# A two-layer decoder trunk in fp32 on one core: other addresses for activation halves and weight halves in SBUF

## The chip, the core and the metric

The program runs on one core of one Trainium2 chip. Its time is the device time of one execution in microseconds (us), as the median of 3 runs; the kernel before takes 2720.65 us (2719.96 to 2721.87).

## What is computed

Two decoder layers on 256 tokens of width 2048, everything in fp32. Each layer is a token mixer, a SwiGLU block and a per-layer input, with RMS norms ahead of and behind them:

```
for i in range(2):
    mix = ssd_mixer(rmsnorm(h), ...) if i == 0 else fox_mixer(rmsnorm(h), ...)
    h = h + rmsnorm(mix)
    ff = (silu(hn @ w_gate) * (hn @ w_up)) @ w_down        # hn = rmsnorm(h), hidden 5632
    h = h + rmsnorm(ff)
    h = h + sigmoid(h @ w_pgate) * rmsnorm(p[i] @ w_proj)  # p[i]: 256 tokens x 256
```

Layer 0's mixer is a state-space one (input projection 2048 x 10304, a convolution, a chunked scan, output projection 4096 x 2048); layer 1's is attention with 16 heads of 128 (input projection 2048 x 6160, output projection 2048 x 2048). There are 125 million weights, used once each.

## The kernel before

**Layout.** Activations lie transposed: 128 channels on the partitions, 256 tokens along the free axis, so 16 tiles hold one activation of width 2048. An fp32 product is made of three products of rounded halves: an activation is split into `x` hi and `x` lo, a weight into `wh` and `wl` (type fp32r), and hi·wh + lo·wh + hi·wl is summed in PSUM.

**Weight stages.** `emit_stage` (from L167) loads one stage of weights, up to 128 x 1024 words, into `raw` (L177, SyncE's DMA queue), casts it to `wh` on ScalarE (L189) and subtracts on VectorE to get `wl` (L194). There are 6 buffers of `raw` and 4 each of `wh` and `wl`.

**Products.** `unit` (from L209) walks through the stages of up to 6 output tiles. The common form is a pair: a *wide* product (L256) that loads 128 columns of `wh` as the stationary operand and streams 512 columns of one activation tile, hi and lo one behind the other, and a *narrow* one (L258) that loads `wl` and streams the 256 columns of hi. While a product streams, the weights of the following one are loaded into TensorE (PEld in the profile). Two other forms exist. In *separate* units (`sep`, L251 to L253; the last unit of every output projection) each pair is three products of 256 columns. In *token* units (`tok`, L245 to L247; the values of the attention layer) the activation is the stationary operand and 412 or 416 columns of weights stream.

**Small products.** L444 to L448 (`filler`) project the per-layer input, in the gaps that the norms leave. Plain fp32 products of the scan, the attention scores and the transposes stand between the units.

**What sets the order.** Python code emits the work unit by unit; lists of small steps (`bg`) are popped between stages; a scheduler then orders the instructions of each engine. Pools decide the addresses: they lie one behind the other in SBUF in the order in which they are opened (L68 to L79). Three pools, `gap_l`, `gap_x` and `gap`, hold nothing but 16, 24 and 56 words of padding (L43 to L45).

**Addresses before.** Counted in fp32 words and modulo 64, and adding up the pools in their order: every tile of `wh` starts at word 8 and every tile of `wl` at 24 (4 x 1024 words and 16 of padding later). The 16 tiles of `h` hold 40 words beside their 16 x 256, so with 24 words of padding every tile of `x` starts at 24 too, and so do the tiles `a` (SwiGLU), `xq` (second half of the scan's output) and `xb` (input of layer 1). The lo half follows the hi half directly, at 24 again, since a half has 4 x 64 words.

**Tiles that the change moves.** `praw` holds `p[i]` (L422) until it is split into `psp` (`part`, L426). `pp` (16 tiles for the projected per-layer input), `gz` (10 buffers, L766) and `pn` (4 buffers, L784) are the per-layer input's and update's own. `dtT`, `adT`, `dtk`, `acT`, `nega` are the scan's step sizes (L820 to L825). `q` and `k` of four heads at a time lie in 12 buffers `qk` (L1340, L1347); the attention outputs `ots` are 16 tiles `x` (L1264), written in `values` (L1319).

Of the kernel before, what the change touches and what calls it, by code (L numbers as in the profile page):

```python
# [41 lines left out]
TAIL_WIDE = 2  # L42
GAP_L = 16  # L43
GAP_X = 24
GAP_A = 56  # L45

_VEC = {}
# [12 lines left out]
def tile_trunk(ctx, tc, a, out):  # L60
# [13 lines left out]
    gap_x = pool(ctx, "gap_x")  # L74
    xp = pool(ctx, "xp", bufs=16)
    ev = pool(ctx, "ev", bufs=2)
# [14 lines left out]
    ones = cp.tile([P, P], F32, name="ones")  # L91
    mhalf = cp.tile([P, 2], F32, name="mhalf")

    def col(name, c=0, n=P):
# [72 lines left out]
    def emit_stage(a_ins=None, v_ins=None):  # L167
        i = len(emitted)
        cols, r, kc, n = stages[i]

        def view(t):
            return t[:, :kc * n].rearrange("p (c n) -> p c n", n=n)

        raw = wp.tile([P, SW], F32, tag="raw", name=f"raw{i}", bufs=RAWB)
        o = 0
        for W, c0, w in cols:
            nc.sync.dma_start(  # L177
                out=view(raw)[:, :, o:o + w],
                in_=W[r:r + kc * P, c0:c0 + w].rearrange("(c p) n -> p c n", p=P))
            o += w  # L180
        wh = whp.tile([P, SW], F32R, tag="wh", name=f"wh{i}", bufs=WB)
        wl = wlp.tile([P, SW], F32R, tag="wl", name=f"wl{i}", bufs=WB)
        if a_ins is None:
            a_ins, turn_a[0] = turn_a[0], None
        with ExitStack() as order:
            for ins in [a_ins] + lag[0]:
                order.enter_context(after(ins))
            lag[:] = [lag[1], []]
            low_a[0] = A.copy(out=wh[:, :kc * n], in_=raw[:, :kc * n])  # L189
        with ExitStack() as order:  # L190
            for ins in [v_ins] + turn:
                order.enter_context(after(ins))
            turn.clear()
            low[0] = V.tensor_tensor(out=wl[:, :kc * n], in0=raw[:, :kc * n],  # L194
                                     in1=wh.bitcast(F32)[:, :kc * n], op=sub)
        emitted.append((view(wh), view(wl), kc))
# [12 lines left out]
    def unit(rhs, evac, tok=False, pre=None, pops=1, late=(), merge=1, look=LOOK, sep=False):  # L209
# [10 lines left out]
        while k0 < K:  # L220
# [12 lines left out]
            with after(p0):  # L233
                p = None
                for t in range(nt):
                    with after(p if ordered else None):
                        for wh, wl, kc, kb in held:
                            for c in range(kc):
# [16 lines left out]
                                else:  # L255
                                    PE.matmul(accs[t], lhsT=wh[:, c, t * P:(t + 1) * P],  # L256
                                              rhs=x.rearrange("p a n -> p (a n)"), start=st, stop=False)
                                    last = PE.matmul(accs[t][:, :T], lhsT=wl[:, c, t * P:(t + 1) * P],  # L258
# [135 lines left out]
    A.dma_start(out=hx[0][:, :T + NCH], in_=a["x0"])  # L394
    x00 = xp.tile([P, 2, T], F32R, tag="x", name=nm("x"))
    V.tensor_scalar(out=x00[:, 0, :], in0=h[0], scalar1=hx[0][:, T:T + 1], scalar2=None, op0=mult)
# [7 lines left out]
    for _ in range(WARM):  # L404
        PE.matmul(wps[:, :P], lhsT=ones, rhs=ones, start=True, stop=True)

    def newx():
        return xp.tile([P, 2, T], F32R, tag="x", name=nm("x"))

# [10 lines left out]

    def load_p(i, mp):
        pr = mp.tile([P, 2, T], F32, tag="praw", name=f"praw{i}")  # L422
        G.dma_start(out=pr, in_=a[f"pT{i}"].rearrange("(c p) n -> p c n", p=P))
        pts.clear()

        def part(c):  # L426
            t = mp.tile([P, 2, T], F32R, tag=f"psp{c}", name=f"psp{i}_{c}")
            placed(pr[:, c, :], t)
            pts.append(t)
        bg.extend((noop, noop, noop, lambda: part(0), lambda: part(1)))  # L430
# [157 lines left out]
    def tail(i, mpx, m, pp, mk_next):  # L588
# [3 lines left out]
        with ExitStack() as st:  # L592
# [38 lines left out]
            for half in range(2):  # L631
                acts = [ap_.tile([P, 2, T], F32R, tag="a", name=nm("a")) for _ in range(HALF)]
                c0 = 0
# [38 lines left out]
        xs2 = [newx() for _ in range(NCH)]  # L672
        next_xs = mk_next() if mk_next is not None else None
        r0 = post_norm(filler(pp, (2, 3)))

# [88 lines left out]
        def e3(t, acc, c0):  # L764
            c = c0 + t
            gz[c] = pn.tile([P, T], F32, tag="gz", name=nm("gz"), bufs=10)  # L766
            gather(acc, gz[c])
# [12 lines left out]
        for u, (n, todo) in enumerate(zip(OUT0, (pops0, pops1, pops2, pops3))):  # L780
            last = u == len(OUT0) - 1
            up = None
            if u == 0:
                up = mk_update(lambda: pn.tile([P, T], F32, tag="pn", name=nm("pn"), bufs=4), m,  # L784
                               f"ffn_post{i}", None, xs2, r0)
# [27 lines left out]
    with ExitStack() as ys:  # L813
        yp = pool(ys, "yp", side="right")
        y = [yp.tile([P, T], F32, name=f"y{c}") for c in range(32)]
        with ExitStack() as st:
            sp = pool(st, "sp")
            dp = pool(st, "dp", space=bass.MemoryType.DRAM)
            acd = dp.tile([NH, T], F32, name="acd")
            dtT = sp.tile([NH, T], F32, name="dtT")  # L820
            adT = sp.tile([NH, T], F32, name="adT")
            dtk = sp.tile([P, 4, NH], F32, name="dtk")
            acT = sp.tile([NH, T], F32, name="acT")
            bias3 = sp.tile([P, 3, NH], F32, name="bias3")
            nega = sp.tile([NH, 1], F32, name="nega")  # L825
            cbm = [sp.tile([P, 384], F32, name=f"cbm{g}") for g in range(NG)]
            s2s = ExitStack()
            s2 = pool(s2s, "s2")
            bT = [s2.tile([P, T], F32, name=f"bT{g}") for g in range(NG)]
            wdt.append(s2.tile([P, NCH * NH], F32, name="wdt"))  # L830
# [272 lines left out]
            def z_unit(g, pops):  # L1103
                S = {}

                def ev_z(t, acc):
# [3 lines left out]
                    if t == 0:  # L1110
                        S["ss"] = yp.tile([P, T], F32, tag="gss", name=nm("gss"), bufs=1)
                        if g == 0:
# [32 lines left out]
            def ysplit(c):  # L1145
                if c not in yts:
                    yts[c] = newx() if c < 16 else xq.tile([P, 2, T], F32R, tag="xq",
                                                           name=nm("xq"))
                    placed(y[c], yts[c])
# [18 lines left out]
        def m0():  # L1168
            if not st0:
# [6 lines left out]
                st0["m"] = [st0["mp"].tile([P, T], F32, name=f"m0_{c}") for c in range(NCH)]  # L1176
                st0["pp"] = [st0["mp"].tile([P, T], F32, name=f"pp0_{c}") for c in range(NCH)]
                load_p(0, st0["mp"])
            return st0["m"]
# [4 lines left out]
    def mk_next():  # L1184
        p_ = pool(xr_s, "xb")
        return [p_.tile([P, 2, T], F32R, tag=f"xb{c}", name=nm("xb")) for c in range(NCH)]
    nxt = tail(0, st0["s"], st0["m"], st0["pp"], mk_next)
# [75 lines left out]
    bg.extend((f1, noop, f2, noop, f3))  # L1263
    ots = [newx() for _ in range(FH)]  # L1264

    RNG = ((0, P), (P, 384))

    def quad_tasks(hds, q, k):
# [50 lines left out]
        def values():  # L1319
            pss = [misc(), misc()]  # L1320

            def mm(i, b):
# [6 lines left out]
                   hds[-1] == FH - 1)  # L1329
            for i in range(4):  # L1330
                split(pss[i // 2][:, (i % 2) * T:(i % 2 + 1) * T], ots[hds[i]])

# [6 lines left out]
    for u in range(4):  # L1339
        q = [fp.tile([P, T], F32, tag="qk", name=nm("q"), bufs=12) for _ in range(4)]  # L1340

# [4 lines left out]
        unit(lambda k: nxt[k], ev_q)  # L1346
        kk = [fp.tile([P, T], F32, tag="qk", name=nm("k"), bufs=12) for _ in range(4)]  # L1347

# [13 lines left out]
    def m1():  # L1362
        if not st1:
# [5 lines left out]
            st1["m"] = [st1["mp"].tile([P, T], F32, name=f"m1_{c}") for c in range(NCH)]  # L1369
            st1["pp"] = [st1["mp"].tile([P, T], F32, name=f"pp1_{c}") for c in range(NCH)]  # L1370
            load_p(1, st1["mp"])
        return st1["m"]
# [72 lines left out]
```

## Time and profile before

| | |
|---|---|
| median of 3 runs | 2720.65 us |
| time of the profiled execution | 2720.78 us |
| its span | 2719.0 us |
| PE (matmul) busy | 2711.1 us, 100% of the span |
| PEld (weight load) busy | 2410.5 us, 89% |
| DVE (VectorE) busy | 1905.3 us, 70% |
| ACT (ScalarE) busy | 1480.7 us, 54% |
| DMA | 519.59 MB, 191 GB/s |

A matmul's end is modelled in the profile and its pipeline overlaps the next one, so a "busy" TensorE says little. What counts is the distance from the start of one product to the start of the next. It is read from the timeline (columns: start in us, length in us, engine, line, operation, output and inputs, how many were merged) or from a table of stretches: a stretch, its length, then the busy time of an engine and in brackets how many of its instructions ran in it, one or two of which reach in over the edge.

### The profile page before, as it was taken

The page shows a single profiled execution, that of the slowest core. Times are in us where ns is not written, and L with a number is a line of the kernel's source. Part 1 is how long each engine was busy: PE and PEld are TensorE (multiplying, and loading weights), DVE is VectorE, ACT ScalarE, POOL GpSimd, SP SyncE. Part 2 cuts the span into 40 slices and gives each one's busy share as a digit, 9 for nine tenths or more (in the row PEclk, how much of TensorE's full clock was granted, in tenths as well). Part 3 has the DMA queues.
Part 4 walks back from the last instruction along what each step waited for, and adds up shares of the span by engine and source line. Part 5 has one row for each costly group of instructions (what it writes and reads, how often), then busy time and mean ns, then how long its engine had stood idle before and what let it go on. Part 6 is the DMA issues. An engine that isn't in the chain of part 4 may idle for free.

```text
span 2719.0 us, 43137 instructions
## 1 busy us (share of the span) xinstructions
PE 2711.1 (100%) x16342; PEld 2410.5 (89%) x16342; DVE 1905.3 (70%) x3147; ACT 1480.7 (54%) x2455; POOL 48.8 (2%) x106
## 2 busy tenths in 40 slices
PE   9999999999999999999999999999999999999999
PEld 8888888889888888888898998889888888888898
DVE  8888888755976645666668656766976646666577
ACT  6577677554655444545456544555654444445454
POOL 0000000000000000000000000000000000000000
PEclk9999999999999999999999999999999999999999
DMA  7666666565666656666556676655666566656655
GB/s 265 186 203 189 191 202 188 159 215 168 188 206 193 193 194 192 193 179 202 199 161 198 184 215 188 185 156 168 203 199 196 189 199 190 198 176 201 202 162 167
DMA packets 262657, 519.59 MB, mean 191 GB/s; under 512 B 17408, under 2 KB 44192, under 8 KB 262448
## 3 DMA queue, kind: packets, MB, share of 16 engines
q1 hardware_dynamic: 258784, 504.54, 60.2%
q0 software_dynamic: 3520, 12.15, 1.5%
q8 instruction: 128, 2.10, 0.3%
q14 instruction: 81, 0.66, 0.1%
q10 hardware_dynamic: 144, 0.14, 0.0%
HBM read 514.58 MB, written 2.18 MB: 190 GB/s over the span
## 4 chain that ended last, share of the span: by engine, by line
PE 97%; DVE 1%; ACT 1%; issue 1%; DMA 0%; DVEq 0%; ACTq 0%
PE acc L256 56%; PE acc L258 29%; PE acc L253 1%; PE acc L252 1%; PE acc L251 1%; PE acc L247 1%; PE acc L246 1%; PE acc L245 1%; PE mi L1012 1%; DVE wl L194 1%; ACT E L992 1%; PE mi L1277 0%; PE mi L1325 0%; ACT wh L189 0%; PE acc L444 0%
## 5 line engine op out<-in xcount | busy, mean ns | idle before, releaser
L256 PE MATMUL acc<-x,wh 128*128 128x512 f32 x4992 | 1673.4, 391 | 0.9 <-DVE gz L285 0.8
L194 DVE TENSOR_TENSOR wl<-raw,wh 128x1024 fp32r<-128x1024 f32 (+4 forms) x1020 | 1169.4, 1152 | 694.0 <-ACT wh L189 688.9
L189 ACT CAST wh<-raw 128x1024 fp32r<-128x1024 f32 (+4 forms) x1020 | 1006.4, 993 | 934.0 <-PE acc L256 800.0
L258 PE MATMUL acc<-x,wl 128*128 128x256 f32 x4992 | 1305.2, 278 | 0.9 <-DVE wl L194 0.7
L256 PEld LDWEIGHTS acc<-x,wh 128*128 128x128 f32 x4992 | 921.8, 188 | 181.8 <-issue 1.3
L258 PEld LDWEIGHTS acc<-x,wl 128*128 128x128 f32 x4992 | 923.0, 188 | 26.4 <-DVE wl L194 3.4
L256 PE MATMUL acc<-a,wh 128*128 128x512 f32 x1232 | 417.5, 389 | 0.0
L258 PE MATMUL acc<-a,wl 128*128 128x256 f32 x1232 | 335.2, 276 | 0.0
L256 PEld LDWEIGHTS acc<-a,wh 128*128 128x128 f32 x1232 | 229.8, 188 | 46.2
L258 PEld LDWEIGHTS acc<-a,wl 128*128 128x128 f32 x1232 | 231.3, 188 | 2.1
L256 PE MATMUL acc<-xb,wh 128*128 128x512 f32 x512 | 176.6, 392 | 0.0
L284 ACT COPY tb<-acc 128x256 f32<-128x256 f32 x400 | 140.5, 370 | 48.6 <-PE acc L258 20.9
L258 PE MATMUL acc<-xb,wl 128*128 128x256 f32 x512 | 142.4, 279 | 0.0
L256 PEld LDWEIGHTS acc<-xb,wh 128*128 128x128 f32 x512 | 95.6, 188 | 19.2
L258 PEld LDWEIGHTS acc<-xb,wl 128*128 128x128 f32 x512 | 96.2, 188 | 0.8 <-issue 0.2
L256 PE MATMUL acc<-xq,wh 128*128 128x512 f32 x224 | 76.3, 389 | 0.0
L908 DVE SCALAR_TENSOR_TENSOR g<-xr,vec,g 128x256 f32<-128x256 f32 x144 | 63.5, 478 | 11.6 <-ACT g L905 11.4
L285 DVE TENSOR_TENSOR g<-acc,tb 128x256 f32<-128x256 f32 x171 | 65.1, 416 | 0.4
L258 PE MATMUL acc<-xq,wl 128*128 128x256 f32 x224 | 61.7, 276 | 0.0
L992 ACT ACTIVATE E<-ab,bias 128x128 f32<-128x128 f32 x192 | 59.9, 393 | 2.5 <-DMA ab<-acd 2.5
L308 DVE TENSOR_TENSOR ssb<-ssb,sq 128x256 f32<-128x256 f32 x120 | 50.6, 422 | 12.4 <-ACT sq L307 8.7
L344 POOL TENSOR_TENSOR rs<-ms,mhalf 128x2 f32<-128x2 f32 x18 | 22.6, 1255 | 1965.7 <-DVE ms L341 1965.7
(228 smaller groups left out, 2160.1 us busy)
## 6 DMA issues: line engine op xcount, KB each, us to landing
raw<-down SPq DMA_DIRECT2D x176, 512.0 KB, 4.2
raw<-ssd_in SPq DMA_DIRECT2D x144, 512.0 KB, 4.5
raw<-gate SPq DMA_DIRECT2D x128, 512.0 KB, 4.2
raw<-up SPq DMA_DIRECT2D x128, 512.0 KB, 4.4
raw<-fox_in SPq DMA_DIRECT2D x64, 512.0 KB, 4.2
raw<-gate SPq DMA_DIRECT2D x64, 384.0 KB, 3.3
raw<-up SPq DMA_DIRECT2D x64, 384.0 KB, 3.5
raw<-ssd_out SPq DMA_DIRECT2D x40, 512.0 KB, 4.1
```

The source lines that it names most:

```text
L189: low_a[0] = A.copy(out=wh[:, :kc * n], in_=raw[:, :kc * n])
L194: low[0] = V.tensor_tensor(out=wl[:, :kc * n], in0=raw[:, :kc * n], in1=wh.bitcast(F32)[:, :kc * n], op=sub)
L245: PE.matmul(o, lhsT=xh, rhs=wh[:, c, :], start=st, stop=False)
L246: PE.matmul(o, lhsT=xh, rhs=wl[:, c, :], start=False, stop=False)
L247: last = PE.matmul(o, lhsT=x[:, 1, t * P:(t + 1) * P], rhs=wh[:, c, :], start=False, stop=sp)
L256: PE.matmul(accs[t], lhsT=wh[:, c, t * P:(t + 1) * P], rhs=x.rearrange("p a n -> p (a n)"), start=st, stop=False)
L258: last = PE.matmul(accs[t][:, :T], lhsT=wl[:, c, t * P:(t + 1) * P], rhs=x[:, 0, :], start=False, stop=sp)
L284: i = A.copy(out=tb[:np_], in_=acc[:np_, T:2 * T])
L285: took[0] = (i, V.tensor_tensor(out=o, in0=acc[:np_, :T], in1=tb[:np_], op=add))
L308: last_v[0] = V.tensor_tensor(out=acc, in0=acc, in1=sq, op=add)
L908: V.scalar_tensor_tensor(out=c, in0=xr[:, k:k + T], scalar=col(f"conv_w{k}", cc), in1=c, op0=mult, op1=add)
L992: A.activation(E[:, i, b * P:(b + 1) * P], ab[:, i, lo:lo + P], AF.Relu, scale=-1.0, bias=bias3[:, b, h0 + i:h0 + i + 1])
```

## The change

All addresses below are in fp32 words modulo 64.

- `xp`, `act`, `xq`, `xb` and `psp` tiles grow from 512 to 576 words (`ROOM_X`), and the lo half starts 308 words behind the hi half (`LOW_X`; 308 = 256 + 52). The wide product's moving operand becomes two runs of 256 words (`[[308, 2], [1, 256]]`) where it was one run of 512.
- `gap_l` grows from 16 to 48 words, and `wl` tiles from 1024 to 1088 words, used from the 4th. So `wl` now starts at 60 (8 + 48 + 4), the hi halves at 56, the lo halves at 44, and `wh` stays at 8: `wh` lies 16 and `wl` 4 words past hi.
- To make room: `p[i]` is loaded by two DMAs into `m[14]` and `m[15]`, which are written only later; `pp[8:16]` is allocated when the SwiGLU tiles are gone; `pn` and `gz` share 11 buffers in place of 4 and 10; `dtk` lives in `rpe`, the sums of squares of the scan's norm in `ssp`; `dtT`, `adT`, `acT`, `nega` live in a pool that closes earlier; `q` and `k` lie in the room of the `x` tiles, four heads a slot group, and the attention outputs come into the same slots after them (`newx` takes a slot number).

```
-GAP_L = 16
+GAP_L = 48
 GAP_X = 24
 GAP_A = 56
+LOW_X = 308
+ROOM_X = 576
+SHIFT_L = 4
+ROOM_L = 64
...
-    xp = pool(ctx, "xp", bufs=16)
+    xp = pool(ctx, "xp")
...
+    def halves(pool_, **kw):
+        t = pool_.tile([P, ROOM_X], F32R, **kw)
+        return bass.AP(t.tensor, t.offset, [list(t.ap[0]), [LOW_X, 2], [1, T]])
+
+    slot = iter(range(1 << 20))
+
+    def newx(c=None):
+        c = next(slot) % NCH if c is None else c
+        return halves(xp, tag=f"x{c}", name=nm("x"))
...
-        wl = wlp.tile([P, SW], F32R, tag="wl", name=f"wl{i}", bufs=WB)
+        wl = wlp.tile([P, SW + ROOM_L], F32R, tag="wl", name=f"wl{i}", bufs=WB)
+        wl = wl[:, SHIFT_L:SHIFT_L + SW]
...
-                                    PE.matmul(accs[t], lhsT=wh[:, c, t * P:(t + 1) * P],
-                                              rhs=x.rearrange("p a n -> p (a n)"), start=st, stop=False)
+                                    PE.matmul(accs[t].rearrange("p (a n) -> p a n", a=2),
+                                              lhsT=wh[:, c, t * P:(t + 1) * P], rhs=x,
+                                              start=st, stop=False)
...
-    def load_p(i, mp):
-        pr = mp.tile([P, 2, T], F32, tag="praw", name=f"praw{i}")
-        G.dma_start(out=pr, in_=a[f"pT{i}"].rearrange("(c p) n -> p c n", p=P))
+    def load_p(i, mp, pr):
+        for c in range(2):
+            G.dma_start(out=pr[c], in_=a[f"pT{i}"][c * P:(c + 1) * P, :])
...
-                acts = [ap_.tile([P, 2, T], F32R, tag="a", name=nm("a")) for _ in range(HALF)]
+                acts = [halves(ap_, tag="a", name=nm("a")) for _ in range(HALF)]
...
+        pp_ = pool(mpx, f"ppb{i}", side="right")
+        pp.extend(pp_.tile([P, T], F32, name=f"ppb{i}_{c}") for c in range(8, NCH))
...
-            gz[c] = pn.tile([P, T], F32, tag="gz", name=nm("gz"), bufs=10)
+            gz[c] = pn.tile([P, T], F32, tag="gz", name=nm("gz"), bufs=11)
...
-                up = mk_update(lambda: pn.tile([P, T], F32, tag="pn", name=nm("pn"), bufs=4), m,
+                up = mk_update(lambda: pn.tile([P, T], F32, tag="gz", name=nm("pn"), bufs=11), m,
...
-            dtk = sp.tile([P, 4, NH], F32, name="dtk")
+            dtk = rpe.rearrange("p (a n) -> p a n", n=NH)
...
-                        S["ss"] = yp.tile([P, T], F32, tag="gss", name=nm("gss"), bufs=1)
+                        S["ss"] = ssp
...
-    ots = [newx() for _ in range(FH)]
+    ots = {}
...
+                ots[hds[i]] = newx(hds[i])
                 split(pss[i // 2][:, (i % 2) * T:(i % 2 + 1) * T], ots[hds[i]])
...
-        q = [fp.tile([P, T], F32, tag="qk", name=nm("q"), bufs=12) for _ in range(4)]
+        qk = [xp.tile([P, ROOM_X], F32, tag=f"x{4 * u + j}", name=nm("qk")) for j in range(4)]
+        q = [o[:, :T] for o in qk]
...
-        kk = [fp.tile([P, T], F32, tag="qk", name=nm("k"), bufs=12) for _ in range(4)]
+        kk = [o[:, T:2 * T] for o in qk]
```

**What it does to the order.** TensorE's and SyncE's lists hold the same instructions in the same order before and after, and VectorE's and ScalarE's differ at one place. That place is the last attention quad (`values` of heads 12 to 15), where ScalarE casts the hi halves of four head outputs (L289, L305 after) and the weight stages that follow (L189, L204 after). ScalarE's list before (`x` is a head's output tile, `mi` the PSUM tile it comes from, `wh` and `raw` a weight stage):

```order
1555 L189 CAST wh_19318<-raw_19316 128x768
1556 L289 CAST x_16998<-mi_19280 128x256
1557 L289 CAST x_16999<-mi_19280 128x256
1558 L289 CAST x_17000<-mi_19281 128x256
1559 L189 CAST wh_19336<-raw_19334 128x768
1560 L289 CAST x_17001<-mi_19281 128x256
1561 L189 CAST wh_19354<-raw_19352 128x768
```

And ScalarE's list after, at the same rows:

```order
1555 L204 CAST wh_19297<-raw_19295 128x768
1556 L305 CAST x_19271<-mi_19256 128x256
1557 L305 CAST x_19274<-mi_19256 128x256
1558 L305 CAST x_19265<-mi_19255 128x256
1559 L305 CAST x_19268<-mi_19255 128x256
1560 L204 CAST wh_19315<-raw_19313 128x768
1561 L204 CAST wh_19333<-raw_19331 128x768
```

The fourth cast of a head has moved ahead of one weight cast; VectorE's subtractions move in the same way.

GpSimd's list, where the per-layer input of layer 0 is loaded (`pT` in memory; `rs` are the small powers of the norms), before:

```order
82 L344 TENSOR_TENSOR rs_5669<-ms_5667,mhalf 128x2
83 L344 TENSOR_TENSOR rs_6081<-ms_6079,mhalf 128x2
84 L423 DMA praw_6632<-pT 128x2x256
85 L344 TENSOR_TENSOR rs_7723<-ms_7721,mhalf 128x2
86 L344 TENSOR_TENSOR rs_8365<-ms_8363,mhalf 128x2
```

And after:

```order
82 L360 TENSOR_TENSOR rs_5661<-ms_5659,mhalf 128x2
83 L360 TENSOR_TENSOR rs_6072<-ms_6070,mhalf 128x2
84 L436 DMA m_14_6605<-pT 128x256
85 L436 DMA m_15_6606<-pT 128x256
86 L360 TENSOR_TENSOR rs_7706<-ms_7704,mhalf 128x2
87 L360 TENSOR_TENSOR rs_8348<-ms_8346,mhalf 128x2
```

One DMA has become two, at the same place between the same powers; the same happens in layer 1.

More of the change, by code (lines that the diff above doesn't have):

```diff
@@ L394, in tile_trunk @@
     A.dma_start(out=hx[0][:, :T + NCH], in_=a["x0"])
-    x00 = xp.tile([P, 2, T], F32R, tag="x", name=nm("x"))
+    x00 = newx()
     V.tensor_scalar(out=x00[:, 0, :], in0=h[0], scalar1=hx[0][:, T:T + 1], scalar2=None, op0=mult)
@@ L405, in tile_trunk @@
         PE.matmul(wps[:, :P], lhsT=ones, rhs=ones, start=True, stop=True)
-    def newx():
-        return xp.tile([P, 2, T], F32R, tag="x", name=nm("x"))
     rwide = cp.tile([P, T], F32, name="rwide")
@@ L419, in tile_trunk @@
     pts, lo_done, held_pp = [], set(), []
-    def load_p(i, mp):
-        pr = mp.tile([P, 2, T], F32, tag="praw", name=f"praw{i}")
-        G.dma_start(out=pr, in_=a[f"pT{i}"].rearrange("(c p) n -> p c n", p=P))
+    def load_p(i, mp, pr):
+        for c in range(2):
+            G.dma_start(out=pr[c], in_=a[f"pT{i}"][c * P:(c + 1) * P, :])
         pts.clear()
         def part(c):
-            t = mp.tile([P, 2, T], F32R, tag=f"psp{c}", name=f"psp{i}_{c}")
-            placed(pr[:, c, :], t)
+            t = halves(mp, tag=f"psp{c}", name=f"psp{i}_{c}")
+            placed(pr[c], t)
             pts.append(t)
@@ L819, in tile_trunk @@
             acd = dp.tile([NH, T], F32, name="acd")
-            dtT = sp.tile([NH, T], F32, name="dtT")
-            adT = sp.tile([NH, T], F32, name="adT")
-            dtk = sp.tile([P, 4, NH], F32, name="dtk")
-            acT = sp.tile([NH, T], F32, name="acT")
+            dtk = rpe.rearrange("p (a n) -> p a n", n=NH)
             bias3 = sp.tile([P, 3, NH], F32, name="bias3")
-            nega = sp.tile([NH, 1], F32, name="nega")
             cbm = [sp.tile([P, 384], F32, name=f"cbm{g}") for g in range(NG)]
@@ L828, in tile_trunk @@
             s2 = pool(s2s, "s2")
+            dtT, adT, acT = (s2.tile([NH, T], F32, name=n) for n in ("dtT", "adT", "acT"))
+            nega = s2.tile([NH, 1], F32, name="nega")
             bT = [s2.tile([P, T], F32, name=f"bT{g}") for g in range(NG)]
@@ L1146, in ysplit @@
                 if c not in yts:
-                    yts[c] = newx() if c < 16 else xq.tile([P, 2, T], F32R, tag="xq",
-                                                           name=nm("xq"))
+                    yts[c] = newx() if c < 16 else halves(xq, tag="xq", name=nm("xq"))
                     placed(y[c], yts[c])
@@ L1176, in m0 @@
                 st0["m"] = [st0["mp"].tile([P, T], F32, name=f"m0_{c}") for c in range(NCH)]
-                st0["pp"] = [st0["mp"].tile([P, T], F32, name=f"pp0_{c}") for c in range(NCH)]
-                load_p(0, st0["mp"])
+                st0["pp"] = [st0["mp"].tile([P, T], F32, name=f"pp0_{c}") for c in range(8)]
+                load_p(0, st0["mp"], st0["m"][14:])
             return st0["m"]
@@ L1185, in mk_next @@
         p_ = pool(xr_s, "xb")
-        return [p_.tile([P, 2, T], F32R, tag=f"xb{c}", name=nm("xb")) for c in range(NCH)]
+        return [halves(p_, tag=f"xb{c}", name=nm("xb")) for c in range(NCH)]
     nxt = tail(0, st0["s"], st0["m"], st0["pp"], mk_next)
@@ L1369, in m1 @@
             st1["m"] = [st1["mp"].tile([P, T], F32, name=f"m1_{c}") for c in range(NCH)]
-            st1["pp"] = [st1["mp"].tile([P, T], F32, name=f"pp1_{c}") for c in range(NCH)]
-            load_p(1, st1["mp"])
+            st1["pp"] = [st1["mp"].tile([P, T], F32, name=f"pp1_{c}") for c in range(8)]
+            load_p(1, st1["mp"], st1["m"][14:])
         return st1["m"]
```

## Prediction

> **What bounds the kernel now.** I read the page first: whose work the span consists of.
>
> ```profile
> span 2719.0 us, 43137 instructions
> ...
> PEclk9999999999999999999999999999999999999999
> ...
> PE 97%; DVE 1%; ACT 1%; issue 1%; DMA 0%; DVEq 0%; ACTq 0%
> ...
> L256 PE MATMUL acc<-x,wh 128*128 128x512 f32 x4992 | 1673.4, 391 | 0.9 <-DVE gz L285 0.8
> L258 PE MATMUL acc<-x,wl 128*128 128x256 f32 x4992 | 1305.2, 278 | 0.9 <-DVE wl L194 0.7
> L256 PE MATMUL acc<-a,wh 128*128 128x512 f32 x1232 | 417.5, 389 | 0.0
> L256 PE MATMUL acc<-xb,wh 128*128 128x512 f32 x512 | 176.6, 392 | 0.0
> L256 PE MATMUL acc<-xq,wh 128*128 128x512 f32 x224 | 76.3, 389 | 0.0
> ```
>
> The chain that ended last is TensorE's for 97% of the span, at a full granted clock, with almost no idle time ahead of its products. There are 4992 + 1232 + 512 + 224 = 6960 pairs of a wide and a narrow product. So the time is the number of products times the distance from one start to the next. I looked for that distance in stretches in which only pairs run, by counting the narrow product L258 (PE and PEld: busy us and count).
>
> ```profile
> 540.00:640.00 100.00, 80.65 (x295) 55.16 (x294) 1.00 0.63 207
> 760.00:1222.00 462.00, 369.68 (x1358) 254.73 (x1357) 1.00 0.63 193
> 1968.00:2420.00 452.00, 361.72 (x1328) 249.13 (x1328) 1.00 0.63 193
> ```
>
> 462 us / 1357 and 452 / 1328 are 0.340 us a pair, over 2600 pairs with hardly an exception. A pair streams 768 columns, so this *clean beat* is 0.4427 ns a column: 226.7 ns for a wide product, 113.3 ns for a narrow one. At it the 6960 pairs need 2366 us. It isn't kept everywhere. The same two lines, in the scan's input projection:
>
> ```profile
> 299.77 0.40 PE L256 MATMUL acc<-x,wh 128*128 128x512 f32 x1
> 300.01 0.28 PE L258 MATMUL acc<-x,wl 128*128 128x256 f32 x1
> 300.12 0.40 PE L256 MATMUL acc<-x,wh 128*128 128x512 f32 x1
> ...
> 300.47 0.40 PE L256 MATMUL acc<-x,wh 128*128 128x512 f32 x1
> ```
>
> Here wide to wide takes 0.35 us, with the same tiles at the same addresses modulo 64 and no idle time: a *slow beat*, 10 ns longer. A third pattern, from the SwiGLU block:
>
> ```profile
> 1299.93 0.28 PE L258 MATMUL acc<-a,wl 128*128 128x256 f32 x1
> 1300.04 0.39 PE L256 MATMUL acc<-a,wh 128*128 128x512 f32 x1
> 1300.27 0.40 PE L258 MATMUL acc<-a,wl 128*128 128x256 f32 x2
> 1300.50 0.39 PE L256 MATMUL acc<-a,wh 128*128 128x512 f32 x1
> ```
>
> Two narrow products in a row take 0.23 us or a little more (2 x 113.3 = 226.7 ns clean). The separate and token units are slow throughout. Their stretches, all of TensorE's products counted:
>
> ```profile
> 653.00:675.00 22.00, 22.00 (x189) 1.00 0.54 156
> 2590.00:2610.00 20.00, 20.00 (x172) 1.00 0.53 169
> 1504.00:1534.00 30.00, 30.00 (x161) 1.00 0.69 186
> ```
>
> Less the two that reach in over an edge: 22 / 187 = 117.6 ns and 20 / 170 = 117.6 ns for a separate product of 256 columns (113.3 clean), 30 / 159 = 188.7 ns for a token product of 412 columns (182.4 clean).
>
> **What can be gained.** I summed by how much each start-to-start distance in the timeline exceeds the clean one. Distances longer by 15 ns or more are left out: waits for weights, and plain fp32 products in between. Over the 13,920 products of L256 and L258 (first and last below) it is 14.4 us; over the 1008 separate, 480 token and 192 filler products, summed alike, 4.5 + 3.0 + 0.9 = 8.4 us (by the rows above, 1008 x 4.3 ns and 480 x 6.3 ns are 4.3 and 3.0).
>
> ```profile
> 5.56 1.40 PE L256 MATMUL acc<-x,wh 128*128 128x512 f32 x5
> ...
> 2703.04 0.28 PE L258 MATMUL acc<-x,wl 128*128 128x256 f32 x1
> ```
>
> So 22.8 us, 0.84% of the span, is all that hangs on something other than counts, waits and the clean beat. Is it a matter of addresses? The best row is in the token units of 416 columns, where the same line L246 streams `wl` from word 56 and from word 24 in turn, under the load of an activation at 24:
>
> ```profile
> 1590.12 0.35 PE L246 MATMUL acc<-wl,xb 128*128 128x416 f32 x1
> 1590.31 0.35 PE L247 MATMUL acc<-wh,xb 128*128 128x416 f32 x1
> ...
> 1590.69 0.35 PE L246 MATMUL acc<-wl,xb 128*128 128x416 f32 x1
> 1590.89 0.35 PE L247 MATMUL acc<-wh,xb 128*128 128x416 f32 x1
> ```
>
> From 56 it takes 0.19 us, from 24 0.20; the pattern repeats with every pair of chunks. Shape, clock and neighbours are alike, only the address differs. I take it that the reading of the stationary columns and the reading of the moving ones get into each other's way at certain distances, and that the two beats above are the same conflict, hit or missed according to the moment at which the load begins.
>
> **The change, part by part.**
>
> *New distances.* During a narrow product `wh` is loaded while hi streams: its distance was 8 - 24 = 48 and becomes 16. During a wide one `wl` is loaded, beginning with hi: 0 becomes 4. In the separate units the three distances were 48, 0, 48 and all become 16 (`wl` against lo: 60 - 44). Modulo 64 is my assumption; the tiles' sizes keep it. No row of before shows a pair at 16 and 4. Bounds: at best every product comes to the clean distance, -22.8 us; at worst every pair takes the slow beat, 6960 x 10 ns = 69.6 us less the 14.4 that are paid already, +55 us. The nearest rows are token products of 412 columns, whose second chunk starts 412 words (28) further on:
>
> ```profile
> 1522.27 0.35 PE L246 MATMUL acc<-wl,xb 128*128 128x412 f32 x1
> 1522.46 0.35 PE L247 MATMUL acc<-wh,xb 128*128 128x412 f32 x1
> 1522.66 0.35 PE L245 MATMUL acc<-wh,xb 128*128 128x412 f32 x1
> 1522.84 0.35 PE L246 MATMUL acc<-wl,xb 128*128 128x412 f32 x1
> ```
>
> The first two stream from 52 and 36 under a load from 24 (distances 36 and 52) and take 0.19 and 0.20 us; the third streams from 8 (distance 16) and takes 0.18. So 16, which `wh` gets, looks good; of 4, which `wl` gets, no row tells. I take a gain, nearer to the best end, because the clean beat is by far the commonest (2685 of the 6960 pairs in the two long stretches alone) and a distance that is the same in all separate products leaves fewer moments to hit: 11 of the 14.4 us for the pairs, 3.5 of the 8.4 for the rest, -14.5 us.
>
> *Two runs in the wide operand.* No row shows TensorE reading a moving operand with a jump inside. Nearest rows: two separate products in place of one cost 2 x 117.6 = 235.2 against 226.7 ns, 8.5 ns, at worst 59 us over 6960; two clean narrow ones cost nothing more than a wide one. I take 0, since the clean rows are nearest (one instruction, no load between the runs), and nothing below 0, as no column is saved.
>
> *Moved tiles.* TensorE's order is unchanged, so each of these only matters if it makes a weight half or an activation late.
>
> ```profile
> 1821.55 0.83 ACT L189 CAST wh<-raw 128x768 fp32r<-128x768 f32 x1 [0.49 <-ACT x L289]
> 1822.28 0.37 ACT L289 CAST x<-mi 128x256 fp32r<-128x256 f32 x1
> 1823.59 0.83 ACT L189 CAST wh<-raw 128x768 fp32r<-128x768 f32 x1 [0.94 <-ACT x L289]
> ...
> 1824.45 0.96 DVE L194 TENSOR_TENSOR wl<-raw,wh 128x768 fp32r<-128x768 f32 x1 [0.74 <-ACT wh L189]
> ```
>
> The cast that moves ahead (0.37 us) delays one weight cast and its subtraction; behind them ScalarE has 0.94 and VectorE 0.74 us idle, which takes it up: 0, at most 0.4 us without that cover.
>
> ```profile
> 560.15 0.76 POOL L423 DMA_DIRECT2D praw<-pT  x1 [41.26 <-DVE xq L300]
> 572.55 0.40 ACT L298 CAST psp<-praw 128x256 fp32r<-128x256 f32 x1
> ```
>
> The second DMA adds one issue of about 0.76 us on GpSimd's queue, ahead of the norms' powers; the first reader starts 12.4 us after the issue: 0, or 0.8 us if the first cast had to wait. `m[14]` and `m[15]` are written only by the last unit, after both casts. Shared `gz`/`pn` buffers, `ppb`, `rpe`, `ssp` and the slots of `q` and `k` are read in an order that puts the old reader ahead of the new writer on TensorE or VectorE anyway: 0 each, with those few tenths as their bound.
>
> Sum: 2719.0 - 14.5 = 2704.5 us span. The profiled execution lies 1.8 us above its span and 0.1 above the median, so I predict **2706 us**, 0.54% less.
>
> **The rivals.**
>
> *Addresses don't matter* (chance 0.17): the slow beat would be a matter of when the sequencer issues a load, and address and chunk in the 416-column rows only go together. The clean and slow beat at the same addresses speak for it. Then the 22.8 us stay: 2721 us, within a few us. The Trainium skill, "TensorE: Matmul & The Clock Gate", section "Step-by-step: what each phase is for", has this as its rule: TensorE reads its moving operand and its weights through two independent ports, and loading the next weights takes no bandwidth from the running matmul. By that rule the sum would be 0; the 0.19 and 0.20 us rows speak against it, and no row of before separates address from moment for the pairs.
>
> *The slow beat becomes the rule* (0.17): at 16 and 4 the load conflicts in most moments. The slow token products above, at 52 and 36, are 4 modulo 16, as the new distance of `wl`; that speaks for it. At half of all pairs it costs 6960 x 0.5 x 10 - 14.4 us = +20: 2741 us; at all 2776. It decides against the change once more than 21% of the pairs (14.4 us / 10 ns / 6960) run slow.
>
> *The jump costs* (0.06): from 2 ns a wide product on (14 us) it eats the gain; at the bound of 8.5 ns the time would be about 2765 us.
>
> *Anything else* (0.04): VectorE's or ScalarE's own accesses get slower or faster at the new addresses, a buffer is awaited; some us either way.
>
> **How the numbers follow.** The forecast has 0.56. Within it the gain runs from a quarter of the 22.8 us (2715) to all of it (2698). A measurement of this kernel can tell about 0.2%, 5.4 us, from no change. Faster by more: 0.54 of the forecast's 0.56 and 0.02 of the rest, 0.56. Within it: 0.16 of the first rival and 0.03 of the others, 0.19. Slower: 0.25, nearly all of the second and third rivals. The range goes from 2697 us, all conflicts gone, to 2742 us, half the pairs at the slow beat; about 0.05 lie below and 0.11 above.
>
> **What would show it.** In the profile after, stretches of pairs at 300 and 2632 us should run at 0.340 us a pair, the separate units at under 116 ns a product and the number of instructions stay, but for two DMAs. If long stretches of SwiGLU (760 to 1222 us before) run at 0.344 or more, the second rival holds; if each wide product there is longer by the same few ns with the narrow one unchanged, the third; if the slow beat and the separate units are as before, the first. A clean beat below 0.340 us would show that I was wrong in taking it as a floor.

## The result, and the profile after

The changed kernel takes 2739.34 us (median of 4 runs, 2738.76 to 2740.92), the kernel before on the same chip 2720.63 us (4 runs, 2719.96 to 2721.87). The ratio is 1.0069, 95% interval 1.0052 to 1.0087: 18.7 us slower, where 2706 us was forecast. The profiled execution took 2740.92 us, of which 2739.1 is span.

The page after has the same lines as before; the costliest groups are the same two, now L271 (wide) and L274 (narrow):

```profile
span 2739.1 us, 43140 instructions
...
PEclk9999999999999999999999999999999999999999
...
PE 96%; DVE 2%; ACT 1%; issue 1%; DMA 0%; ACTq 0%; DVEq 0%
...
L271 PE MATMUL acc<-x,wh 128*128 128x512 f32 x4992 | 1687.9, 393 | 1.7 <-DVE gz L301 0.8
...
L274 PE MATMUL acc<-x,wl 128*128 128x256 f32 x4992 | 1312.1, 279 | 1.0 <-DVE wl L209 0.7
...
L271 PE MATMUL acc<-a,wh 128*128 128x512 f32 x1232 | 424.7, 392 | 0.0
```

The clock and the counts of products are as before, and the chain and the idle time ahead of the products nearly so (1.7 and 1.0 us, 0.9 each before). The products themselves have become longer: 1687.9 us for the wide ones of `x` in place of 1673.4, 1312.1 in place of 1305.2 for the narrow ones. Where, the table of stretches tells, the narrow product L274 alone (PE and PEld: busy us and count):

```profile
540.00:640.00 100.00, 80.26 (x289) 54.17 (x289) 1.00 0.63 205
760.00:1222.00 462.00, 368.02 (x1335) 250.42 (x1334) 1.00 0.63 190
1968.00:2420.00 452.00, 358.93 (x1307) 244.89 (x1306) 1.00 0.63 193
```

These are the stretches that held the clean beat before, with 294, 1357 and 1328 pairs. Now 462 us / 1334 = 0.3463 and 452 / 1306 = 0.3461 us a pair. The timeline of TensorE inside SwiGLU shows it one by one:

```profile
899.84 0.39 PE L271 MATMUL acc<-x,wh 128*128 128x512 f32 x1
900.07 0.28 PE L274 MATMUL acc<-x,wl 128*128 128x256 f32 x1
900.19 0.39 PE L271 MATMUL acc<-x,wh 128*128 128x512 f32 x1
...
901.23 0.39 PE L271 MATMUL acc<-x,wh 128*128 128x512 f32 x1
```

From the first to the last row it is four pairs in 1.39 us, 0.347 us each, with no wait: both products of a pair are some ns late, pair after pair. Some stretches go the other way. One of the two that the prediction names, at 2632 us, before (L258 alone):

```profile
2632.00:2653.00 21.00, 16.83 (x61) 11.26 (x61) 1.00 0.65 206
```

Less one that reaches in over an edge, 21 us / 60 = 0.350 us a pair. The same pairs after, now at 2652 us (first and last wide product of 60):

```profile
2652.43 0.39 PE L271 MATMUL acc<-x,wh 128*128 128x512 f32 x1
...
2672.49 0.39 PE L271 MATMUL acc<-x,wh 128*128 128x512 f32 x1
```

59 distances in 20.06 us are 0.340 each: here the change does what was forecast. In the other, around 300 us (the 82 pairs that start from 290 to 320 us before), it does not: 342.4 ns a pair before, 342.9 after, waits left out. The separate units improve too. All of TensorE's products in a stretch of the second output projection:

```profile
2610.00:2628.00 18.00, 18.00 (x161) 1.00 0.55 176
```

Less the two that reach in over an edge, 18 / 159 = 113.2 ns a product, where it was 117.6: these units are clean now.

The same sum as in the prediction, each start-to-start distance less the clean one (for the plain fp32 products the distance itself), in us of the two profiled executions:

| | before | after |
|---|---|---|
| pairs, below 15 ns each | 14.4 | 38.0 |
| separate units | 4.5 | 0.3 |
| token units | 3.0 | 2.9 |
| filler | 0.9 | 0.2 |
| 15 ns or more (waits) | 21.3 | 22.7 |
| fp32 products | 75.0 | 75.3 |

The differences add up to +20.3 us, with their rounding; the spans differ by 20.1. So the loss is one term, +23.6 us in the pairs. There are 6374 places where a narrow product stands right behind a wide one. From the start of the wide one to whatever follows the narrow one 5168 of them took 340 ns before, and 1641 do after; 4151 take 346 or 347. Which it is goes with the last irregularity ahead, counted in the same timeline from the third pair behind it: behind two wide products in a row 311 of 319 pairs took at most 341 ns, behind two narrow ones in a row 3232 of 3600 took 346 or 347. In the kernel before, 3560 of the 3600 behind two narrow ones took at most 341.

### The profile page after: what moved, and what is told of

Read it like the earlier page. It is cut to its first block, busy times and chain, and to the rows that moved or that the text cites. A ratio compares the mean times of both kernels' runs of the same rounds, so it can differ in the third digit from the quotient of the medians.

```text
span 2739.1 us, 43140 instructions
## 1 busy us (share of the span) xinstructions
PE 2730.2 (100%) x16342; PEld 2419.8 (88%) x16342; DVE 1905.3 (70%) x3147; ACT 1481.6 (54%) x2455; POOL 50.4 (2%) x108
## 4 chain that ended last, share of the span: by engine, by line
PE 96%; DVE 2%; ACT 1%; issue 1%; DMA 0%; ACTq 0%; DVEq 0%
PE acc L271 56%; PE acc L274 29%; PE acc L267 1%; PE acc L266 1%; PE acc L268 1%; PE acc L261 1%; PE acc L260 1%; PE acc L262 1%; PE mi L1025 1%; DVE wl L209 1%; ACT E L1005 0%; ACT wh L204 0%; PE mi L1289 0%; PE mi L1337 0%; DMA ab<-acd 0%
## 5 line engine op out<-in xcount | busy, mean ns | idle before, releaser
L271 PE MATMUL acc<-x,wh 128*128 128x512 f32 x4992 | 1687.9, 393 | 1.7 <-DVE gz L301 0.8
L204 ACT CAST wh<-raw 128x1024 fp32r<-128x1024 f32 (+4 forms) x1020 | 1006.4, 993 | 959.1 <-PE acc L271 834.1
L274 PE MATMUL acc<-x,wl 128*128 128x256 f32 x4992 | 1312.1, 279 | 1.0 <-DVE wl L209 0.7
L271 PEld LDWEIGHTS acc<-x,wh 128*128 128x128 f32 x4992 | 922.2, 188 | 187.8 <-DVE gz L301 1.5
L274 PEld LDWEIGHTS acc<-x,wl 128*128 128x128 f32 x4992 | 923.3, 188 | 27.5 <-DVE wl L209 3.9
L271 PE MATMUL acc<-a,wh 128*128 128x512 f32 x1232 | 424.7, 392 | 0.0
L274 PE MATMUL acc<-a,wl 128*128 128x256 f32 x1232 | 339.3, 280 | 0.0
L271 PEld LDWEIGHTS acc<-a,wh 128*128 128x128 f32 x1232 | 229.9, 188 | 48.9
L274 PEld LDWEIGHTS acc<-a,wl 128*128 128x128 f32 x1232 | 231.3, 188 | 2.2
L271 PE MATMUL acc<-xb,wh 128*128 128x512 f32 x512 | 177.6, 393 | 0.0
L274 PE MATMUL acc<-xb,wl 128*128 128x256 f32 x512 | 142.8, 280 | 0.0
L271 PEld LDWEIGHTS acc<-xb,wh 128*128 128x128 f32 x512 | 95.7, 188 | 19.7
L274 PEld LDWEIGHTS acc<-xb,wl 128*128 128x128 f32 x512 | 96.2, 188 | 0.9 <-issue 0.2
L271 PE MATMUL acc<-xq,wh 128*128 128x512 f32 x224 | 77.7, 392 | 0.0
L921 DVE SCALAR_TENSOR_TENSOR g<-xr,vec,g 128x256 f32<-128x256 f32 x144 | 63.3, 477 | 12.1 <-ACT g L918 11.9
L274 PE MATMUL acc<-xq,wl 128*128 128x256 f32 x224 | 62.6, 280 | 0.0
```

Of the source, the lines that this page charges most:

```text
L271: PE.matmul(accs[t].rearrange("p (a n) -> p a n", a=2), lhsT=wh[:, c, t * P:(t + 1) * P], rhs=x, start=st, stop=False)
L921: V.scalar_tensor_tensor(out=c, in0=xr[:, k:k + T], scalar=col(f"conv_w{k}", cc), in1=c, op0=mult, op1=add)
```

## The experiments

**Which distance, and is it the distance at all?** Four kernels differ from the changed one in one or two constants; TensorE's list is the same instructions in the same order in all of them. Below, 16/4 stands for `wh` 16 and `wl` 4 words past hi modulo 64, and a third number for the words from hi to lo: the kernel before is 48/0/256, the changed one 16/4/308. The old distances, with the new homes and the jump:

```
-GAP_L = 48
+GAP_L = 16
-SHIFT_L = 4
+SHIFT_L = 0
```

> The changed kernel with the weights' distances of before (wh 48, wl 0 past hi), but the lo half 308 words behind hi and all tiles in their new homes. Distances theory: the SwiGLU pairs come back to 340 ns as before, 2716 to 2721 us, the separate units (48, 52, 48 now) anywhere between 113 and 118 ns. Jump theory: the slow beat stays, 2735 to 2740 us. Moved tiles: 2739 us.

Measured 2718.57 us, ratio to before 0.9992 (0.9983 to 1.0001). The new distances without the jump:

```
-LOW_X = 308
+LOW_X = 256
```

> The changed kernel with the lo half directly behind the hi half again (one run of 512 in the wide product); wl still 4 and wh 16 words past hi, all tiles in their new homes. Distances theory (the pair's slow beat of 346.5 ns comes from loading wl at 4 or wh at 16): the SwiGLU pairs stay at 346.5 ns and the separate units, whose distances are 16, 4 and 16 now, lose part of their gain: 2739 to 2744 us. Jump theory (the wide product pays for its two runs): the pairs come back to 340 ns: about 2716 to 2720 us. Moved tiles: no change, 2739 us, with the waits of 15 ns and more as they are.

Measured 2724.49 us, 1.0015 (1.0006 to 1.0024). Only `wl` back at 0:

```
-SHIFT_L = 4
+SHIFT_L = 0
```

> The changed kernel with wl 4 words earlier: wl 0 and wh 16 words past hi. Distances theory, wl at fault: SwiGLU pairs at 340 ns, about 2716 to 2722 us. Distances theory, wh at fault: pairs stay at 346.5 ns, 2738 to 2744 us. Jump theory and moved tiles: 2739 us.

Measured 2750.85 us, 1.0111 (1.0094 to 1.0128). Only `wh` back at 48:

```
-GAP_L = 48
+GAP_L = 16
```

> The changed kernel with hi at word 24 and wl at 28: wh 48 and wl 4 words past hi. Distances theory, wl at fault: slow beat in the SwiGLU pairs, 2738 to 2744 us. Distances theory, wh at fault: pairs at 340 ns, 2716 to 2722 us. Jump theory and moved tiles: 2739 us.

Measured 2764.53 us, 1.0162 (1.0147 to 1.0177). The narrow product in SwiGLU, first with the old distances:

```profile
760.00:1222.00 462.00, 368.36 (x1357) 254.55 (x1356) 1.00 0.61 193
```

without the jump:

```profile
760.00:1222.00 462.00, 369.59 (x1354) 254.21 (x1354) 1.00 0.60 192
```

with `wl` at 0:

```profile
760.00:1222.00 462.00, 367.37 (x1346) 252.99 (x1345) 1.00 0.60 192
```

and with `wh` at 48:

```profile
760.00:1222.00 462.00, 363.34 (x1325) 248.13 (x1325) 1.00 0.59 189
```

That is 0.3407, 0.3412, 0.3435 and 0.3487 us a pair. With the old distances everything is back, so moved tiles, the two DMAs and the jump by itself cost nothing. My theory that one of the two weight halves is at fault falls: putting either one back alone makes it worse than both new. And the jump, free at 48/0, makes 15 us of difference at 16/4. Three addresses count together: `wh`, `wl` and lo, each seen from hi.

**A probe.** So I measured the pairs by themselves, in bursts from constant tiles with no other engine at work. Each of the four probes ran once.

> A probe that computes nothing of the model: TensorE runs bursts of pairs (a wide product of 512 columns under a wh column block, a narrow one of 256 under a wl block) from constant tiles, 160 settings one after the other: the low half 256, 276, 292 or 308 words behind the high half, wh at a distance of 0, 8, 16, 32 or 48 words past hi modulo 64, wl at 0, 4, 8, 12, 16, 24, 32 or 48. In each setting 24 pairs behind two fp32 products, 24 behind two narrow products in a row, 24 behind two wide ones in a row, then 24 separate products. No other engine touches the memory. Three theories. Combination theory: the beat hangs on wh, wl and the low half's distance together, with several self-keeping beats: 48/0/256 and 48/0/308 at 0.340 us a pair in nearly all pairs, 16/4/308 at 0.345 or more, 16/4/256 between them, 48/4/308 and 16/0/308 at 0.350 or more. Each-by-itself theory: the excess of a setting is a term for wh plus a term for wl, alike at all four places of the low half. Program theory: addresses act only through what the other engines do in the same memory at the same time; then all 160 settings run at 0.340 us.

No burst of the 480 settled at 340 ns: in their second halves they ran at 343 to 356 ns, all but 8 of them at 346 or more. The setting labelled 48/0/308, its second burst (timeline of TensorE; first and last wide product of 24):

```profile
4418.88 0.39 PE L62 MATMUL acc<-xs,wh 128*128 128x512 f32 x1
...
4426.93 0.39 PE L62 MATMUL acc<-xs,wh 128*128 128x512 f32 x1
```

23 pairs in 8.05 us, 0.350 each. This fitted none of the three theories as I had put them, so I looked for what the probe lacked:

> The first probe never held 0.340 us a pair: 348 to 354 ns in 158 of its 160 settings. Its tiles all lay within 21 KB of each partition; in the model kernels wh, wl and the activations lie 16 and 32 KB apart. This probe, which computes nothing of the model either, runs 90 settings: activations, wh and wl as far apart as in the model kernels with the low half 256 or 308 words behind the high one, and close together with 256; wh at 0, 4, 16, 32, 48 and wl at 0, 4, 8, 16, 32, 48 past hi. Per setting 3 x 32 pairs in the model kernels' order of chunks and accumulators (behind fp32 products, two narrow ones, two wide ones), then 24 separate products. Place theory: far apart, 48/0/256 runs at 0.340 us a pair and 16/4/308 at 0.345 to 0.347, close together all at 0.348 or more. Order theory: it was the accumulation or the step from one column block to the next, so near and far are alike, with 48/0 at 0.340. Program theory: near and far stay at 0.348 or more, and what keeps the beat at 0.340 in the model kernels is something the probe has not got, such as the semaphore events on the products.

Place was not it: 48/0 ran at 340.0 ns behind all three beginnings, far apart at 256 and at 308 and close together at 256, and 28 of the 30 settings at 256 agreed between far and near to 0.1 ns; the other two, 0/0 and 0/4, had bursts at 353.3 ns far and at 346.7 near. (By the second halves 159 of the first probe's 160 settings lie between 346 and 354 ns, where the expectation says 348 to 354 for 158.) 16/4/308 had two beats, 346.7 ns behind the fp32 products and 340.0 behind the other two beginnings, and its separate products took 113.4 ns. So the place in SBUF played no part in 28 of the 30 settings, and it takes no other engine to bring the two beats about.

> Two questions to the probe, which again computes nothing of the model; tiles close together, low half 308 words behind the high one, per setting 3 x 20 pairs (behind fp32 products, two narrow, two wide) and 24 separate products. First the whole grid: wh and wl each at 0, 4, ... 60 past hi, 256 settings. If the beat is a matter of lucky distances, few settings hold 0.340 us a pair behind all three beginnings (48/0 is one, 16/4 only behind some), and 113.3 ns in the separate products is as rare and falls on other settings (16/4 among them); a rule of distances modulo 16 words would show the same rows four times, at 0, 16, 32 and 48. Second, why the first probe never held 0.340 at 48/0: its products each opened a new accumulation, and its column blocks followed 128 words apart instead of 512. Four kinds of each of 48/0, 16/4, 48/4 and 16/0. Accumulation theory: the kinds called fresh are slow (0.348 or more at 48/0) at both steps, the accumulating ones are not. Step theory: the kinds with 128 are slow at both ways of accumulating.

Fresh or accumulating, 128 or 512 words from block to block: 48/0 ran at 340.0 ns in all four kinds, 48/4 at 353.3. What was wrong with the first probe was its own layout: its activation tile was 2648 words, 24 more than a multiple of 64, so that `wh` and `wl` lay 24 words further on than the labels say. Its "48/0/308" is 8/24, and the grid's 8/24 shows the first probe's beats, 350.0, 350.0 and 346.7 ns. None of its settings had `wh` at 16 or 48. The grid's timeline, bursts behind two narrow products, first and last wide product of 20, at 16/4, 16/36, 48/0 and 48/4:

```profile
1636.07 0.39 PE L60 MATMUL acc<-xs,wh 128*128 128x512 f32 x1
...
1642.66 0.39 PE L60 MATMUL acc<-xs,wh 128*128 128x512 f32 x1
...
1832.44 0.40 PE L60 MATMUL acc<-xs,wh 128*128 128x512 f32 x1
...
1838.91 0.39 PE L60 MATMUL acc<-xs,wh 128*128 128x512 f32 x1
...
4766.88 0.39 PE L60 MATMUL acc<-xs,wh 128*128 128x512 f32 x1
...
4773.34 0.39 PE L60 MATMUL acc<-xs,wh 128*128 128x512 f32 x1
...
4791.20 0.40 PE L60 MATMUL acc<-xs,wh 128*128 128x512 f32 x1
...
4797.91 0.40 PE L60 MATMUL acc<-xs,wh 128*128 128x512 f32 x1
```

19 pairs in 6.59, 6.47, 6.46 and 6.71 us: 0.347, 0.341 (its first pairs are late, the rest hold 0.340), 0.340 and 0.353 us each. Over the whole grid, second half of each burst:

| settings (wh/wl past hi, lo at 308) | count of 256 |
|---|---|
| 0.340 us behind all three beginnings: 16/36, 48/0, 48/60 | 3 |
| 0.340 us behind some: 16/0, 16/4, 16/60, 48/36 | 4 |
| 0.340 us behind none | 249 |

The setting 16/4 is slow there behind two narrow products alone (346.7 ns), as in the changed kernel; in the second probe with lo at 308, and in all four kinds, it was slow behind the fp32 products instead. So what a burst begins with does not by itself decide between two beats. The mean of all 768 bursts is 349.7 ns. Separate products came under 113.8 ns at three settings, 16/4, 16/24 and 16/56. Nothing repeats with 16 words: at wl 0, wh 0, 16, 32 and 48 give 349, 351, 352 and 340 ns.

> The grid left three settings that hold 0.340 us a pair behind all three beginnings: wh/wl at 16/36, 48/0 and 48/60; 16/4 holds it only behind some. The probe once more (nothing of the model is computed): bursts of 20, 5, 8, 4, 10, 7, 6 and 20 pairs, with two narrow or two wide products in a row between them, then 48 separate products. 54 settings two words apart around these three at 308, and these three and 16/4 with the low half from 256 to 316 words behind the high one. If the good settings are single points of the grid, two words to either side bring 0.346 or more; if they are wide, their neighbours stay at 0.340. If the low half's distance does not enter into a pair that holds the beat, 16/36, 48/0 and 48/60 stay near 0.340 at all 16 distances, as 48/0 did at 256 and 308; if it enters, only some hold it. The separate products, which read the low half by themselves, should depend on it in either case: 113.3 ns at few distances, 117.7 or more at the others.

The good settings are points. The series of bursts behind the first two narrow products costs 72 ns over the clean distance at 16/36, 94 at 48/0 and 180 at 48/60. Of the other 51 settings at 308 the best are 16/60, 16/4 and 16/0 (267, 385 and 404 ns), which the grid knows as good behind some beginnings; two words to either side of the three in `wl` it is 460 or more, and every setting with wh at 14, 18, 46 or 50 is above 440. And lo enters: of 16 places of lo, 16/36 stays under 100 ns at 296 and 308 alone, 48/0 at 256 and 308 alone, 16/4 at 268 alone (73 ns, separate products 120.0 ns). The series at 16/4 and at 16/36, from the first wide product behind the first two narrow ones to the first separate product (L75):

```profile
527.44 0.39 PE L55 MATMUL acc<-xs,wh 128*128 128x512 f32 x1
...
549.24 0.40 PE L75 MATMUL acc<-xs,wh 128*128 128x256 f32 x2
...
597.60 0.40 PE L55 MATMUL acc<-xs,wh 128*128 128x512 f32 x1
...
619.09 0.39 PE L75 MATMUL acc<-xs,wh 128*128 128x256 f32 x2
```

The same products take 21.80 us at one and 21.49 at the other.

**Back in the kernel.** Two single constants, with what the probe says of them:

```
-SHIFT_L = 4
+SHIFT_L = 36
```

> The changed kernel with wl 36 words past hi instead of 4 (wh 16, low half 308): the one setting of the probe's grid with the smallest excess behind disturbances (72 ns in a series of bursts, where 16/4 had 385 and 48/0 94) and 115.6 ns in the separate products. Distances theory, as the probe has it: the excess of the pairs falls from 38.0 us in the changed kernel to about the 12 us of the old distances or less, the separate products keep some 2.3 ns each (2.3 us); 2713 to 2717 us, 0.1 to 0.3% below the kernel before and the fastest so far. Program theory (the probe's beats do not carry over to a program with other engines at work): anywhere between 2718 and 2765 us, as the other four places.

```
-LOW_X = 308
+LOW_X = 268
```

> The changed kernel with nothing changed but the low half's distance, 268 words instead of 308; wh 16 and wl 4 past hi stay. In the probe 16/4 holds 0.340 us a pair at 268 (excess 73 ns in the series, 385 at 308), and its separate products take 120.0 ns there (113.4 at 308). Distances theory with three distances: 2716 to 2722 us, the pairs' excess near 12 us, the separate products' near 6.7. Theory of a conflict between wh, wl and hi alone: the low half does nothing for the pairs, 2739 us and some us more for the separate products. Program theory: anywhere from 2718 to 2765 us.

Measured 2716.46 us, ratio 0.9986 (0.9977 to 0.9994), and 2720.49 us, 1.0000 (0.9990 to 1.0009); before on the same chip 2720.34 (21 runs). Both are where the distances theory put them. The narrow product in SwiGLU with `wl` at 36:

```profile
760.00:1222.00 462.00, 368.50 (x1360) 255.03 (x1360) 1.00 0.61 193
```

and with lo at 268:

```profile
760.00:1222.00 462.00, 369.91 (x1358) 254.78 (x1357) 1.00 0.60 193
```

1360 and 1357 pairs in 462 us, 0.340 us each, in place of 1334: nothing but lo's place, 40 words nearer, brings the time from 2739.34 back to 2720.49 us. With `wl` at 36 the kernel is 0.14% faster than before, the best of all that were run.

Probe and kernel side by side: the excess of the probe's series, and of the kernels' pairs and separate products by the sum used above.

| wh/wl/lo | probe, series, ns | kernel, pairs, us | probe, separate, ns | kernel, separate, us | kernel's time, us |
|---|---|---|---|---|---|
| 16/36/308 | 72 | 11.9 | 115.6 | 2.5 | 2716.46 |
| 16/4/268 | 73 | 12.3 | 120.0 | 6.5 | 2720.49 |
| 48/0/308 | 94 | 12.1 | 118.2 | 4.5 | 2718.57 |
| 48/0/256 (before) | 94 | 14.4 | 117.8 | 4.5 | 2720.63 |
| 16/4/256 | 234 | 18.5 | 117.8 | 4.4 | 2724.49 |
| 16/4/308 (after) | 327 to 385 | 38.0 | 113.4 | 0.3 | 2739.34 |
| 16/0/308 | 404 | 48.5 | 119.1 | 5.8 | 2750.85 |
| 48/4/308 | 718 | 64.7 | 117.8 | 2.5 | 2764.53 |

The pairs stand in the same order in both, but for 12.3 and 12.1 us. The times of the separate products agree in all rows but the last (117.8 - 113.3 = 4.5 ns for 1007 distances is 4.5 us; in the grid, behind other bursts, 48/4 had 114.0 ns).

## Why the prediction was wrong

- *The bound* was right: the span is the number of products times their distance; no burst and no long stretch ran below the clean beat of 0.340 us a pair.
- *New distances*, the step that failed: "I take a gain, nearer to the best end, because the clean beat is by far the commonest". It was the commonest in a kernel that sat on 48/0, one of the three good settings of the grid's 256, and good with lo at 256 too. Over the grid 0.340 us is the exception (16 of 768 bursts) and 0.3497 the mean. By this map the right starting point for a new pair of distances was a slow beat, with a small chance of the clean one. The term was -11 us for the pairs and measured +23.6. That `wh` at 16 looked good from the token rows was half right (in every burst of the second and third probe that held 0.340 us, `wh` lies at 16 or 48), but the verdict hangs on three addresses together, and the trace of before shows one combination.
- *The second rival* came true: at 16 and 4 the slow beat is the rule, in about three quarters of the pairs. That it is the load that conflicts is not shown. Its size was off, since this setting's slow beat is 346.7 ns, not 350: at 6.7 ns a pair the change starts to lose at 14.4 us / 6.7 ns / 6960 = 31% of the pairs in place of 21%. Its reason, slow distances that are 4 modulo 16, was wrong: the grid shows no such rule, `wl` at 4 is clean with lo at 268, and `wl` at 36 makes the fastest kernel.
- *The separate units, token units and filler* were sized about right: -3.5 us forecast, -4.2 - 0.1 - 0.7 = -5.0 measured. The reason given, a distance that is the same in all three products, doesn't stand, so the gain there was luck. In the grid 16 settings have the same distance in all three; 16/4 is the only clean one of them, and the other 15 took 116.8 to 120.2 ns, past the first three products.
- *Two runs in the wide operand*: 0 was right for the reading itself (2718.57 us with the jump at 48/0). But the jump moves lo, and lo's place decides the beat at 16/4: 2724.49, 2720.49 and 2739.34 us with lo at 256, 268 and 308. I had costed the jump as an instruction and not as a third distance.
- *Moved tiles*: 0 was right. Waits grew by 1.4 us in the changed kernel, and the old distances with all the new homes are not slower than before.
- *Addresses don't matter*: excluded. The same instructions in the same order took from 2716.46 to 2764.53 us with other addresses. The Trainium skill, "TensorE: Matmul & The Clock Gate", section "Step-by-step: what each phase is for", says that the moving operand and the weights come through two independent ports and that loading takes no bandwidth from the running matmul. The probe's grid, with TensorE alone at work, shows 340 to 360 ns for the same pair, which that rule does not account for.

Not settled: whether it is the two readings that get in each other's way, as the prediction took it, and where; why 16 and 48 serve and 0 and 32 don't; and what in the products before picks between two beats of one setting. The runs give a map, not a rule; most settings were tried with lo at 308 alone, and distances that are not even, and lo beyond 316 words, not at all.

## What to carry to other kernels

Where a kernel runs at the distance of its products, a beat that holds over thousands of products can be a property of its addresses, and a change of layout draws a new one: price it from the spread over many layouts, not from the beat that the kernel happens to have. A probe of a few ms with the products alone can rank the layouts: here it put eight in the kernels' order but for one near tie, two of them before their kernels had run. Give it bursts with irregularities between them, since some settings have two beats, and check its real addresses before believing its labels. Take operands that are read at the same time as one setting, all addresses together, and then look for a single constant that repairs it.

## What the runs showed of the hardware

- Pairs of 768 streamed columns settle into beats: of the 768 bursts of the grid 16 lie at 340 ns, and the commonest single values are 346.7 (167) and 353.3 ns (127), 6.7 ns apart; the rest lie between 343 and 360. Some settings have two beats, and what a burst begins with does not by itself decide: 16/0/308 ran at 340.0 ns behind two narrow products and at 357 ns behind the other two beginnings in the grid, and the other way about in the second probe, 356.8 ns behind two narrow ones and 340.0 behind the others.
- In the changed kernel two beats are seen too. The timeline behind a place with two wide products in a row, up to two narrow ones in a row and on from there:

```profile
800.79 0.62 PE L271 MATMUL acc<-x,wh 128*128 128x512 f32 x2
801.25 0.28 PE L274 MATMUL acc<-x,wl 128*128 128x256 f32 x1
801.36 0.39 PE L271 MATMUL acc<-x,wh 128*128 128x512 f32 x1
801.59 0.28 PE L274 MATMUL acc<-x,wl 128*128 128x256 f32 x1
801.70 0.39 PE L271 MATMUL acc<-x,wh 128*128 128x512 f32 x1
...
802.72 0.39 PE L271 MATMUL acc<-x,wh 128*128 128x512 f32 x1
...
803.63 0.40 PE L274 MATMUL acc<-x,wl 128*128 128x256 f32 x2
803.87 0.39 PE L271 MATMUL acc<-x,wh 128*128 128x512 f32 x1
...
805.95 0.39 PE L271 MATMUL acc<-x,wh 128*128 128x512 f32 x1
```

From 801.36 to 802.72 us it is four pairs in 1.36 us, the clean 0.340; behind the two narrow products at 803.63 us it is six pairs in 2.08 us, and the beat of 0.347 is back, as in the rows at 900 us.
